# The triangular substitution of two delta-net heads on 32 partitions, in a new order of heads, scans and products

## The chip, the core and the metric

The kernel runs on one core of one Trainium2 chip. The metric is the device time of one execution in microseconds (us); lower is better. The engines are TensorE (PE in the profile; PEld are its weight loads), VectorE (DVE), ScalarE (ACT), GpSimd (POOL) and SyncE (SP), which issues the transfers. Each engine works through its own queue in order; semaphores hold an instruction back until what it needs is there.

## The reference

One decoder layer on 512 tokens of width 2048, all in float32: a norm, one projection that feeds three mixers (stick-breaking attention with 6 heads, 4 gated convolution groups, a gated delta net with 6 heads), an output projection, and an MLP. What the change touches is the delta net:

```python
def gated_delta_rule(q, k, v, g, beta):
    ...
    m = jnp.where(strict, jnp.einsum('bhnid,bhnjd->bhnij', k_beta, k) * decay, 0.0)
    eye = jnp.eye(C, dtype=f32)
    t_mat = lax.linalg.triangular_solve(eye + m, jnp.broadcast_to(eye, m.shape),
                                        left_side=True, lower=True, unit_diagonal=True)
    u = t_mat @ v_beta
    w = t_mat @ (k_beta * jnp.exp(g)[..., None])
    ...
    def step(state, xs):
        q_c, k_c, u_c, w_c, a_c, gl_c = xs
        v_new = u_c - w_c @ state
        o = q_c @ state + a_c @ v_new
        state = state * jnp.exp(gl_c)[..., None, None] + jnp.swapaxes(k_c, -1, -2) @ v_new
        return state, o
```

For every head and every chunk of tokens a unit triangular matrix is inverted, and then a scan runs over the chunks, each step on the state of the one before.

## The kernel before

Products of float32 matrices are made as three matmuls of rounded parts: `wload` (L94 to L104) loads a weight tile `raw`, ScalarE rounds it to `whi` (L102), VectorE takes the rest `wlo` (L103), and `mm3` (L108 to L110) multiplies `whi` and `wlo` with the parts of the activations. `raw`, `whi` and `wlo` have four buffers each. A whole product of 512 tokens and 128 columns is `gemm`: 4 weight tiles, 48 matmuls, one PSUM buffer `mm` out of three (`MMB`), held until its reader has evacuated it.

The delta net takes 128 tokens as a chunk, so 4 chunks a head (`NB`). Per head h:

- `gdn_in(h)`: three products (k, q, v), a convolution, norms, and the 128x128 matrices `MT` (to be inverted) and `AT` of each chunk. `kq` and `MT` have three buffers, so the fourth head in line waits for the end of the first one's scan.
- `gdn_base(h)` (L406 to L476): the sixteen 32x32 diagonal blocks of the four chunks are gathered through DRAM (`sm`, then `Bq`) so that each lies on one partition: 16 partitions, 1024 elements. There VectorE inverts all sixteen at once in 31 steps of two instructions (L429, L431), 62 instructions a head, of up to 256 elements a partition. The result goes through DRAM again (`sy`) to `Xc`, and five small rounds of 32x32 and 64x64 matmuls on PSUM tag `b`, each evacuated by ScalarE or VectorE, put the full inverse together in `MT`.
- `gdn_scan(h)` (after `gdn_kdec`): for each chunk a chain of matmuls on PSUM tag `s` and small rows: `s`, `bp` (VectorE, L491), `s`, `vn` (ScalarE, L496), `s`, `Sn` (VectorE, L504), and so on to the next chunk; then a norm of the head (L519 to L523) and transposes on PSUM tag `o` (L526).
- `gdn_gate(h)`: one product for the output gate.

The four convolution groups (`sc_group(g)`, three products each) have no part in the delta net; they and the gates fill TensorE while VectorE inverts and scans. What the program says in sequence is not yet the order of the engines: a scheduler takes the instructions of the whole program with their priorities (base and scan are raised by `CPRIO` = 2000, weight loads by `WPRIO` = 400) and with its own estimates of time, and fixes the order of each engine's queue. The attention follows the delta net, with `sb_qk(0)` (two products) first.

Of the kernel before, what the change touches and what calls it, by code (L numbers as in the profile page):

```python
# [11 lines left out]
F32 = mybir.dt.float32  # L12
F32R = mybir.dt.float32r
AF = mybir.ActivationFunctionType
ALU = mybir.AluOpType

P = 128
T = 512
NB = T // P
# [15 lines left out]
CPRIO = 2000  # L35
# [18 lines left out]
def trunk(ctx, tc, xT, wv1, wv2, wa, wo, wu, wd, vec, wf, out, dbg=None):  # L54
    nc = tc.nc
# [126 lines left out]
    for k in range(KT):  # L182
# [3 lines left out]
        a = big()  # L186
# [50 lines left out]
    for c in range(2):  # L237
        t = tmp()
# [164 lines left out]
        V.tensor_tensor(out=q4(kdec), in0=q4(p), in1=edec[:, :, h:h + 1].broadcast_to([P, NB, P]), op=ALU.mult)  # L403
        heads[h]["kdec"] = kdec

    def gdn_base(h):  # L406


        MT = heads[h]["MT"]
        if not gb:  # L410
            gb.update(Bq=gt([P, 32, 32], "Bq"), Yq=gt([P, 32, 32], "Yq"), tq=gt([P, 256], "tq"),
                      Xc=gt([P, 256], "Xc"))
            G.memset(gb["Xc"], 0.0)
        Bq, Yq, tq, Xc = (gb[n] for n in ("Bq", "Yq", "tq", "Xc"))
        p0 = 32 * (h % 2)
        sm = dr.tile([P, NB, P], F32, name="sm", tag="sm", bufs=2)
        nc.sync.dma_start(out=sm, in_=q4(MT))
        for s in range(NB):
            nc.sync.dma_start(
                out=Bq[p0 + 4 * s:p0 + 4 * s + 4],  # L420
                in_=sm[32 * s:32 * s + 32, :, 32 * s:32 * s + 32].rearrange("a k b -> k a b"))
        B, Y, t = Bq[p0:p0 + 16], Yq[p0:p0 + 16], tq[p0:p0 + 16]
        Yf = Y.rearrange("p a b -> p (a b)")
        G.memset(Yf, 0.0)
        G.memset(Yf[:, 0:1024:33], 1.0)
        for i in range(31, 0, -1):
            n = 32 - i
            tv = t[:, :i * n].rearrange("p (a b) -> p a b", a=i)
            V.tensor_tensor(out=tv, in0=B[:, 0:i, i:i + 1].broadcast_to([16, i, n]),  # L429
                            in1=Y[:, i:i + 1, i:32].broadcast_to([16, i, n]), op=ALU.mult)  # L430
            V.tensor_tensor(out=Y[:, 0:i, i:32], in0=Y[:, 0:i, i:32], in1=tv, op=ALU.subtract)  # L431
        sy = dr.tile([16, 32, 32], F32, name="sy", tag="sy", bufs=2)
        nc.sync.dma_start(out=sy, in_=Y)
        Xv = q4(Xc)
        for s in range(NB):
            nc.sync.dma_start(
                out=Xv[32 * s:32 * s + 32, :, 32 * (s % 2):32 * (s % 2) + 32],
                in_=sy[4 * s:4 * s + 4].rearrange("k a b -> a k b"))
        X0 = gt([P, 256], "X0")
        V.transpose(out=X0, in_=Xc)  # L440
        p = xps("b")
        pv = q4(p[:, :128])
        for b in range(NB):
            for s in (0, 64):
                PE.matmul(pv[s + 32:s + 64, b], lhsT=q4(MT)[s:s + 32, b, s + 32:s + 64],
                          rhs=q4(X0)[s:s + 32, b, 0:32], start=True, stop=True)
        A1 = gt([P, 128], "A1")
        S.copy(out=A1[32:64], in_=p[32:64, :128])
        V.tensor_copy(out=A1[96:128], in_=p[96:128, :128])
        p = xps("b")  # L450
        pv = q4(p[:, :128])
        for b in range(NB):
            for s in (32, 96):
                PE.matmul(pv[s - 32:s, b], lhsT=q4(A1)[s:s + 32, b], rhs=Xv[s:s + 32, b, 32:64], start=True, stop=True)
        for s in (0, 2):
            r = slice(32 * s, 32 * s + 32)
            if s:
                V.tensor_scalar(out=Xv[r, :, 32:64], in0=pv[r], scalar1=-1.0, scalar2=None, op0=ALU.mult)
            else:
                S.mul(out=Xv[r, :, 32:64], in_=pv[r], mul=-1.0)  # L460
        lo, hi = slice(0, 64), slice(64, P)
        p = xps("b")
        for b in range(NB):
            PE.transpose(p[lo, b * 64:b * 64 + 64], Xc[lo, b * 64:b * 64 + 64], ident[lo, lo])
        X1 = gt([P, 256], "X1")
        S.copy(out=X1[lo], in_=p[lo, :256])
        p = xps("b")
        for b in range(NB):
            PE.matmul(q4(p[:, :256])[hi, b], lhsT=q4(MT)[lo, b, hi], rhs=q4(X1)[lo, b], start=True, stop=True)
        S.copy(out=X1[hi], in_=p[hi, :256])  # L470
        for r in (lo, hi):
            V.tensor_copy(out=q4(MT)[r, :, r], in_=Xv[r])
        p = xps("b")
        for b in range(NB):
            PE.matmul(q4(p[:, :256])[lo, b], lhsT=q4(X1)[hi, b], rhs=Xv[hi, b], start=True, stop=True)
        S.mul(out=q4(MT)[lo, :, hi], in_=q4(p[:, :256])[lo], mul=-1.0)  # L476
# [161 lines left out]
    def base(h):  # L638
        with tc.high_priority(CPRIO):
            gdn_base(h)  # L640

    def scan(h):
        with tc.high_priority(CPRIO):
            gdn_kdec(h)
            gdn_scan(h)

    gdn_in(0)
    base(0)
    gdn_in(1)
    scan(0)  # L650
    sc_group(0)
    base(1)
    gdn_in(2)
    scan(1)
    gdn_gate(0)
    base(2)
    gdn_in(3)
    scan(2)
    base(3)
    scan(3)  # L660
    gdn_in(4)
    base(4)
    gdn_gate(1)
    gdn_gate(2)
    gdn_in(5)
    scan(4)
    base(5)
    gdn_gate(4)
    sc_group(1)
    gdn_gate(3)  # L670
    sc_group(2)
    sc_group(3)
    scan(5)
    gdn.__exit__(None, None, None)
# [351 lines left out]
```

## Time and profile before

| what | us |
|---|---|
| median of 3 runs (lowest, highest) | 2260.18 (2259.96, 2262.76) |
| the profiled execution | 2259.93 |
| its span, first to last instruction | 2257.9 |
| mean granted TensorE clock, share of full speed | 0.995 |
| PEld, ACT, POOL busy | 1834.4, 914.6, 208.7 |
| DMA: mean over the span | 101 GB/s |

The page gives busy time and share of each engine, and the span in 40 equal slices of 56 us with a busy share in tenths. Tables by stretch give, for each stretch from A to B in us, its length and then busy time and count of each engine, the granted clock, the DMA share and GB/s. A row of the timeline is: start, duration, engine, line, operation, what is written <- what is read, shape, count, and in brackets how long the engine stood idle before it and what ended that. A group of instructions shows its count, busy time, mean in ns, and idle time before it. A wait is: who waited for whom, us in total, times, the longest.

The delta net lies at about 50 to 500 us, the attention at 500 to 780 us, the output projection and the MLP behind.

### The profile page before, as it was taken

How to read it: one execution, taken by the hardware profiler on the slowest of the kernel's cores; microseconds unless marked ns; L12 is line 12 of the kernel's file. 1: busy time of each engine (PE TensorE's matmuls, PEld its weight loads, DVE VectorE, ACT ScalarE, POOL GpSimd, SP SyncE). 2: the span in 40 equal slices, each digit the busy share in tenths (PEclk: the TensorE clock that was granted, in tenths of full speed). 3: DMA queues.
4: the chain of work that ended last, by engine and by line, in shares of the span. 5: the costliest groups of instructions: out<-in, count | busy, mean ns of one | idle time of the engine just before them, and what ended most of it. 6: DMA issues, size and time to landing. Idle time of an engine off the chain costs nothing.

```text
span 2257.9 us, 28036 instructions
## 1 busy us (share of the span) xinstructions
PE 2212.8 (98%) x10394; PEld 1834.4 (81%) x10394; DVE 1646.0 (73%) x2216; ACT 914.6 (41%) x1479; POOL 208.7 (9%) x205
## 2 busy tenths in 40 slices
PE   8999989999999999999999999999999999999998
PEld 7877777788989888788888888888888888888886
DVE  7798999854656743468787787787878878878774
ACT  5524544333434533433333333333333333333334
POOL 4323323101000111000000000000000000000003
PEclk9999999999999999999999999999999999999999
DMA  6332222333222343433433333333333243333332
GB/s 184 97 87 82 72 73 72 87 87 93 82 87 80 89 126 117 134 109 90 124 90 107 108 90 118 96 102 117 88 113 103 89 123 92 102 113 89 116 113 80
DMA packets 112504, 227.05 MB, mean 101 GB/s; under 512 B 18448, under 2 KB 20624, under 8 KB 112368
## 3 DMA queue, kind: packets, MB, share of 16 engines
q1 hardware_dynamic: 112368, 225.26, 33.8%
q8 instruction: 82, 1.34, 0.3%
q14 instruction: 54, 0.44, 0.1%
HBM read 218.53 MB, written 6.68 MB: 100 GB/s over the span
## 4 chain that ended last, share of the span: by engine, by line
PE 89%; DVE 7%; issue 1%; DMA 1%; ACT 1%; SPq 0%; POOL 0%; ACTq 0%; DVEq 0%; POOLq 0%
PE mm L108 19%; PE mm L109 19%; PE mm L110 19%; PE pp L110 8%; PE pp L108 8%; PE pp L109 8%; DVE Yq L431 2%; DVE tq L429 1%; DVE wlo L103 1%; PE mm L268 1%; PE mm L269 1%; PE mm L267 1%; DVE cv L337 1%; DVE big L189 0%; DMA xr<-in_xT_dram 0%
## 5 line engine op out<-in xcount | busy, mean ns | idle before, releaser
L102 ACT CAST whi<-raw 128x512 fp32r<-128x512 f32 (+1 forms) x544 | 333.0, 613 | 619.1 <-PE mm L109 569.5
L103 DVE TENSOR_TENSOR wlo<-raw,whi 128x512 fp32r<-128x512 f32 (+1 forms) x544 | 381.0, 701 | 233.4 <-ACT whi L102 227.3
L868 DVE TENSOR_TENSOR xq<-pp,xq 128x1024 f32<-128x1024 f32 x240 | 290.8, 1222 | 203.1 <-PE pp L110 200.6
L108 PE MATMUL mm<-big,whi 128*128 128x512 f32 x1024 | 406.4, 397 | 0.2 <-DVE y L558 0.2
L110 PE MATMUL mm<-big,wlo 128*128 128x512 f32 x1024 | 405.2, 396 | 0.2
L109 PE MATMUL mm<-big,whi 128*128 128x512 f32 x1024 | 404.4, 395 | 0.0
L108 PE MATMUL mm<-xw,whi 128*128 128x512 f32 x1024 | 398.8, 389 | 0.0
L110 PE MATMUL mm<-xw,wlo 128*128 128x512 f32 x1024 | 398.3, 389 | 0.0
L109 PE MATMUL mm<-xw,whi 128*128 128x512 f32 x1024 | 398.3, 389 | 0.0
L778 ACT CAST W<-q 128x1024 fp32r<-128x1024 f32 x210 | 220.8, 1051 | 399.4 <-PE pp L110 398.1
L108 PE MATMUL pp<-W,A 128*128 128x512 f32 x840 | 326.8, 389 | 0.0
L109 PE MATMUL pp<-W,A 128*128 128x512 f32 x840 | 326.8, 389 | 0.0
L110 PE MATMUL pp<-W,A 128*128 128x512 f32 x840 | 326.8, 389 | 0.0
L779 DVE TENSOR_TENSOR W<-q,W 128x1024 fp32r<-128x1024 f32 x210 | 255.5, 1216 | 5.3 <-ACT W L778 5.3
L110 PEld LDWEIGHTS mm<-big,wlo 128*128 128x128 f32 x1024 | 193.7, 189 | 40.6 <-DVE wlo L103 1.0
L108 PEld LDWEIGHTS mm<-big,whi 128*128 128x128 f32 x1024 | 194.0, 190 | 39.9 <-DVE y L558 0.4
L109 PEld LDWEIGHTS mm<-big,whi 128*128 128x128 f32 x1024 | 194.1, 190 | 39.7 <-DVE big L709 0.3
L108 PEld LDWEIGHTS mm<-xw,whi 128*128 128x128 f32 x1024 | 192.2, 188 | 40.3 <-issue 0.2
L109 PEld LDWEIGHTS mm<-xw,whi 128*128 128x128 f32 x1024 | 192.2, 188 | 40.1 <-issue 0.2
L110 PEld LDWEIGHTS mm<-xw,wlo 128*128 128x128 f32 x1024 | 192.0, 188 | 39.9
L110 PEld LDWEIGHTS pp<-W,A 128*128 128x128 f32 x840 | 157.8, 188 | 32.8
L109 PEld LDWEIGHTS pp<-W,A 128*128 128x128 f32 x840 | 157.6, 188 | 32.8
(264 smaller groups left out, 2226.3 us busy)
## 6 DMA issues: line engine op xcount, KB each, us to landing
raw<-in_wu_dram SPq DMA_DIRECT2D x256, 256.0 KB
q<-in_wd_dram SPq DMA_DIRECT2D x128, 512.0 KB
raw<-in_wa_dram SPq DMA_DIRECT2D x192, 256.0 KB
raw<-in_wo_dram SPq DMA_DIRECT2D x64, 256.0 KB
xr<-in_xT_dram SPq DMA_DIRECT2D x32, 256.0 KB
raw<-in_wv_dram SPq DMA_DIRECT2D x16, 256.0 KB
out_dram<-xq SPq DMA_DIRECT2D x16, 256.0 KB
raw<-in_wv_dram SPq DMA_DIRECT2D x16, 134.0 KB
```

What stands on the lines that cost most here:

```text
L102: S.copy(out=hi[:, :n], in_=raw[:, :n])
L103: V.tensor_tensor(out=lo[:, :n], in0=raw[:, :n], in1=hi[:, :n].bitcast(F32), op=ALU.subtract)
L108: PE.matmul(p, lhsT=lh, rhs=rh, start=first, stop=False, skip_group_check=more)
L109: PE.matmul(p, lhsT=lh, rhs=rl, start=False, stop=False, skip_group_check=more)
L110: PE.matmul(p, lhsT=ll, rhs=rh, start=False, stop=last, skip_group_check=more)
L267: PE.matmul(o, lhsT=xw[k][:, 0, s], rhs=hi[:, ws], start=k == 0 and b % 2 == 0, stop=False)
L268: PE.matmul(o, lhsT=xw[k][:, 0, s], rhs=lo[:, ws], start=False, stop=False)
L269: PE.matmul(o, lhsT=xw[k][:, 1, s], rhs=hi[:, ws], start=False, stop=k == KT - 1 and b % 2 == 1)
L431: V.tensor_tensor(out=Y[:, 0:i, i:32], in0=Y[:, 0:i, i:32], in1=tv, op=ALU.subtract)
L778: S.copy(out=o[:, 0], in_=src)
L779: V.tensor_tensor(out=o[:, 1], in0=src, in1=o[:, 0].bitcast(F32), op=ALU.subtract)
L868: V.tensor_tensor(out=x, in0=p, in1=x, op=ALU.add)
```

## The change

A new function `gdn_sub(h)` gathers the blocks of heads h and h + 1 into 32 neighbouring partitions, inverts all 32 blocks with one set of 62 instructions (32 partitions, the same elements per partition), and writes one `sy` for both. `gdn_base(h)` keeps what follows from `sy`. The calls are put in an order by pairs: two heads' `gdn_in`, then their `sub`, then bases and scans, with the gates and convolution groups moved between them. Lines from L436 of before on stand four lines later in the new file; the two instructions of the substitution (L429, L431) are now L428 and L430.

```diff
-    def gdn_base(h):
-        MT = heads[h]["MT"]
+    def gdn_sub(h):
...
-        p0 = 32 * (h % 2)
-        sm = dr.tile([P, NB, P], F32, name="sm", tag="sm", bufs=2)
-        nc.sync.dma_start(out=sm, in_=q4(MT))
-        for s in range(NB):
-            nc.sync.dma_start(
-                out=Bq[p0 + 4 * s:p0 + 4 * s + 4],
-                in_=sm[32 * s:32 * s + 32, :, 32 * s:32 * s + 32].rearrange("a k b -> k a b"))
-        B, Y, t = Bq[p0:p0 + 16], Yq[p0:p0 + 16], tq[p0:p0 + 16]
+        p0 = 32 * (h // 2 % 2)
+        B, Y, t = (gb[n][p0:p0 + 32] for n in ("Bq", "Yq", "tq"))
+        for g in range(2):
+            sm = dr.tile([P, NB, P], F32, name="sm", tag="sm", bufs=2)
+            nc.sync.dma_start(out=sm, in_=q4(heads[h + g]["MT"]))
+            for s in range(NB):
+                nc.sync.dma_start(
+                    out=B[16 * g + 4 * s:16 * g + 4 * s + 4],
+                    in_=sm[32 * s:32 * s + 32, :, 32 * s:32 * s + 32].rearrange("a k b -> k a b"))
...
-            V.tensor_tensor(out=tv, in0=B[:, 0:i, i:i + 1].broadcast_to([16, i, n]),
-                            in1=Y[:, i:i + 1, i:32].broadcast_to([16, i, n]), op=ALU.mult)
+            V.tensor_tensor(out=tv, in0=B[:, 0:i, i:i + 1].broadcast_to([32, i, n]),
+                            in1=Y[:, i:i + 1, i:32].broadcast_to([32, i, n]), op=ALU.mult)
             V.tensor_tensor(out=Y[:, 0:i, i:32], in0=Y[:, 0:i, i:32], in1=tv, op=ALU.subtract)
-        sy = dr.tile([16, 32, 32], F32, name="sy", tag="sy", bufs=2)
+        sy = dr.tile([32, 32, 32], F32, name="sy", tag="sy", bufs=2)
         nc.sync.dma_start(out=sy, in_=Y)
+        heads[h]["sy"], heads[h + 1]["sy"] = sy[0:16], sy[16:32]
+
+    def gdn_base(h):
+        MT, sy, Xc = heads[h]["MT"], heads[h]["sy"], gb["Xc"]
...
     gdn_in(0)
+    gdn_in(1)
+    sub(0)
+    sc_group(0)
     base(0)
-    gdn_in(1)
+    gdn_in(2)
     scan(0)
...
+    sub(4)
+    gdn_gate(3)
+    sc_group(2)
     base(4)
-    gdn_gate(1)
-    gdn_gate(2)
-    gdn_in(5)
     scan(4)
     base(5)
     gdn_gate(4)
-    sc_group(1)
-    gdn_gate(3)
-    sc_group(2)
     sc_group(3)
     scan(5)
```

The whole list of calls is now: in 0, in 1, sub 0, group 0, base 0, in 2, scan 0, base 1, gate 0, scan 1, in 3, sub 2, gate 1, group 1, base 2, in 4, scan 2, base 3, gate 2, scan 3, in 5, sub 4, gate 3, group 2, base 4, scan 4, base 5, gate 4, group 3, scan 5.

How this moves the engines' queues is seen at two places near the end of the delta net. The numbers behind the names tell one buffer from another; `s_` and `b_` are the PSUM buffers of scan and base, `mm_` those of the products. First TensorE, before, at the base of head 5 and the scan of head 4:

```order
L108 MATMUL mm_4696<-big_119,whi_4699 128x512
L109 MATMUL mm_4696<-big_119,whi_4699 128x512
L489 MATMUL s_3975<-Sn_3967,kq_3108 128x128
L110 MATMUL mm_4696<-big_119,wlo_4700 128x512
L108 MATMUL mm_4696<-big_143,whi_4699 128x512
L109 MATMUL mm_4696<-big_143,whi_4699 128x512
L110 MATMUL mm_4696<-big_143,wlo_4700 128x512
L454 MATMUL b_4110<-Xc_918,A1_4107 32x32 x8
L108 MATMUL mm_4696<-big_169,whi_4699 128x512
L109 MATMUL mm_4696<-big_169,whi_4699 128x512
L110 MATMUL mm_4696<-big_169,wlo_4700 128x512
```

The same place of the changed kernel, the base of head 4 with the scan that follows it and the base of head 5:

```order
L458 MATMUL b_4326<-Xc_1239,A1_4323 32x32 x8
L468 MATMUL b_4337<-ident_78,Xc_1239 64x64 x4
L473 MATMUL b_4344<-X1_4342,MT_3289 64x64 x4
L479 MATMUL b_4352<-Xc_1239,X1_4342 64x64 x4
L498 MATMUL s_4365<-y_3268,MT_3289 128x128
L503 MATMUL s_4369<-vn_4367,kdec_4358 128x128
L512 MATMUL o_4373<-vn_4367,y_3288 128x128
L493 MATMUL s_4376<-Sn_4371,kq_3078 128x128
L449 MATMUL b_4445<-X0_4443,MT_3905 32x32 x8
L498 MATMUL s_4380<-bp_4378,MT_3289 128x128
L458 MATMUL b_4457<-Xc_1239,A1_4454 32x32 x8
L503 MATMUL s_4384<-vn_4382,kdec_4358 128x128
```

Before, two or more product matmuls (and elsewhere some 20) stand between two steps; now the steps follow each other. This goes on for 37 rows, to the third chunk of head 5's scan, before the next product, `mm_5137`, begins.

Second VectorE. Before, at the end of head 5's substitution (`tq`, `Yq`), with the evacuations of a convolution group's first and second product (`tmp_4612<-mm_4539`, `tmp_4688<-mm_4615`):

```order
L431 TENSOR_TENSOR Yq_916<-Yq_916,tq_917 16x31
L545 TENSOR_TENSOR tmp_4612<-mm_4539,R_525 128x512
L103 TENSOR_TENSOR wlo_4673<-raw_4670,whi_4672 128x512
L440 STREAM_TRANSPOSE X0_4096<-Xc_918 128x256
L103 TENSOR_TENSOR wlo_4700<-raw_4697,whi_4699 128x512
L103 TENSOR_TENSOR wlo_4718<-raw_4715,whi_4717 128x512
L504 SCALAR_TENSOR_TENSOR Sn_3967<-Sn_3952,elast_576,s_3965 128x128
L515 SCALAR_TENSOR_TENSOR y_3298<-o_3969,posg_582,oi_3972 128x128
L449 COPY A1_4107<-b_4098 32x128
L103 TENSOR_TENSOR wlo_4736<-raw_4733,whi_4735 128x512
L550 TENSOR_TENSOR tmp_4688<-mm_4615,tmp_4612 128x512
```

Now, in the substitution of heads 4 and 5, with the evacuation of the second product of the last group (`tmp_4721<-mm_4648`) and of the third product of the group before it (`y_4229<-mm_4234`):

```order
L430 TENSOR_TENSOR Yq_1237<-Yq_1237,tq_1238 32x13x19
L428 TENSOR_TENSOR tq_1238<-Bq_1236,Yq_1237 32x240
L559 SCALAR_TENSOR_TENSOR y_4229<-tmp_4226,vc_70,y_4229 128x512
L430 TENSOR_TENSOR Yq_1237<-Yq_1237,tq_1238 32x12x20
L554 TENSOR_TENSOR tmp_4721<-mm_4648,tmp_4645 128x512
L559 SCALAR_TENSOR_TENSOR y_4229<-tmp_4226,vc_70,y_4229 128x512
L428 TENSOR_TENSOR tq_1238<-Bq_1236,Yq_1237 32x231
L430 TENSOR_TENSOR Yq_1237<-Yq_1237,tq_1238 32x11x21
L428 TENSOR_TENSOR tq_1238<-Bq_1236,Yq_1237 32x220
L430 TENSOR_TENSOR Yq_1237<-Yq_1237,tq_1238 32x10x22
L562 TENSOR_TENSOR y_4229<-mm_4234,y_4229 128x512
```

The evacuation of a second product stood behind the whole substitution before, among splits `wlo`; now two evacuations stand in the middle of one, with 22 substitution rows still to come behind the first of them and one split only in the 25 rows before them.

More of the change, by code (lines that the diff above doesn't have):

```diff
@@ L413, in gdn_base @@
             G.memset(gb["Xc"], 0.0)
-        Bq, Yq, tq, Xc = (gb[n] for n in ("Bq", "Yq", "tq", "Xc"))
-        p0 = 32 * (h % 2)
-        sm = dr.tile([P, NB, P], F32, name="sm", tag="sm", bufs=2)
-        nc.sync.dma_start(out=sm, in_=q4(MT))
-        for s in range(NB):
-            nc.sync.dma_start(
-                out=Bq[p0 + 4 * s:p0 + 4 * s + 4],
-                in_=sm[32 * s:32 * s + 32, :, 32 * s:32 * s + 32].rearrange("a k b -> k a b"))
-        B, Y, t = Bq[p0:p0 + 16], Yq[p0:p0 + 16], tq[p0:p0 + 16]
+        p0 = 32 * (h // 2 % 2)
[7 more added lines that the diff above has]
+                    in_=sm[32 * s:32 * s + 32, :, 32 * s:32 * s + 32].rearrange("a k b -> k a b"))
         Yf = Y.rearrange("p a b -> p (a b)")
@@ L645, in scan, with sub @@
             gdn_scan(h)
+    def sub(h):
+        with tc.high_priority(CPRIO):
+            gdn_sub(h)
     gdn_in(0)
+    gdn_in(1)
+    sub(0)
+    sc_group(0)
     base(0)
-    gdn_in(1)
+    gdn_in(2)
     scan(0)
-    sc_group(0)
     base(1)
-    gdn_in(2)
+    gdn_gate(0)
     scan(1)
-    gdn_gate(0)
+    gdn_in(3)
+    sub(2)
+    gdn_gate(1)
+    sc_group(1)
     base(2)
-    gdn_in(3)
+    gdn_in(4)
     scan(2)
     base(3)
+    gdn_gate(2)
     scan(3)
-    gdn_in(4)
+    gdn_in(5)
+    sub(4)
+    gdn_gate(3)
+    sc_group(2)
     base(4)
-    gdn_gate(1)
-    gdn_gate(2)
-    gdn_in(5)
     scan(4)
```

## The prediction

> **What bounds the kernel now.** I read the engine totals first, then the slices, then one table of stretches around the delta-net stage (about 50 to 500 us).
>
> ```profile
> PE 2212.8 (98%) x10394; PEld 1834.4 (81%) x10394; DVE 1646.0 (73%) x2216; ACT 914.6 (41%) x1479; POOL 208.7 (9%) x205
> ...
> PE   8999989999999999999999999999999999999998
> ...
> DVE  7798999854656743468787787787878878878774
> ```
>
> TensorE is busy 98% of the span, so little can be won. Its few weak slices after the start lie in the delta-net stage, just where VectorE shows 8 and 9. The table of stretches gives the size:
>
> ```profile
> core 0: us, PE busy (x) PEld busy (x) DVE busy (x) ACT busy (x) POOL busy (x), PEclk, DMA share, GB/s
> 50.00:150.00 100.00, 100.00 (x454) 82.88 (x454) 79.41 (x142) 49.86 (x96) 34.86 (x32) 1.00 0.31 92
> 150.00:225.00 75.00, 68.19 (x360) 52.89 (x359) 63.21 (x130) 30.09 (x60) 18.31 (x20) 0.95 0.31 88
> 225.00:300.00 75.00, 69.44 (x343) 55.20 (x341) 68.43 (x132) 35.27 (x69) 28.85 (x24) 1.00 0.27 75
> 300.00:350.00 50.00, 43.88 (x223) 35.22 (x223) 47.47 (x84) 24.72 (x51) 14.63 (x13) 0.97 0.22 64
> 350.00:425.00 75.00, 70.89 (x370) 57.19 (x371) 65.39 (x142) 32.46 (x67) 20.82 (x20) 0.95 0.29 82
> 425.00:525.00 100.00, 99.22 (x536) 81.46 (x536) 64.84 (x134) 34.18 (x72) 10.91 (x9) 1.00 0.32 87
> ```
>
> From 150 to 525 us TensorE idles 6.81 + 5.56 + 6.12 + 4.11 + 0.78 = 23.4 us. After its longer waits the granted clock falls: (1 - 0.95) x 75, (1 - 0.97) x 50 and (1 - 0.95) x 75 add up to 9.0 us. So at most **32.4 us** can be won here. The view of waits says who is late:
>
> ```profile
> PE s L494 <- DVE bp L491: 8.3, 4, 3.9
> PE b L445 <- DVE X L440: 5.2, 2, 3.5
> PE s L489 <- DVE Sn L504: 2.7, 2, 2.5
> ```
>
> VectorE's short scan and base rows stand in a queue full of substitution rows. Note also the last stretch, 425 to 525: the tail of the stage costs almost nothing (0.78 us), because products stand between its chain steps.
>
> **The change part by part.** First, the substitution itself:
>
> ```profile
> L103 DVE TENSOR_TENSOR wlo<-raw,whi 128x512 fp32r<-128x512 f32 x135 | 97.1, 720 | 36.0 <-ACT whi L102 32.0 <-ACT rtok L135 2.6 <-DMA raw<-in_wa_dram 0.3
> L431 DVE TENSOR_TENSOR Yq<-Yq,tq 16x31 f32<-16x31 f32 (+15 forms) x186 | 83.8, 450 | 4.6
> L429 DVE TENSOR_TENSOR tq<-Bq,Yq 16x31 f32<-16x31 f32 (+15 forms) x186 | 81.5, 438 | 10.1 <-DMA Bq<-sm 5.5
> ...
> L555 DVE SCALAR_TENSOR_TENSOR y<-tmp,vc,y 128x512 f32<-128x512 f32 x6 | 5.9, 1001 | 1.4 <-ACT y L553 1.4
> ...
> 139.63 0.41 DVE L431 TENSOR_TENSOR Yq<-Yq,tq 16x252 f32<-16x252 f32 x1
> ...
> 144.57 0.40 DVE L393 TENSOR_TENSOR y<-i,g 128x256 f32<-128x256 f32 x1
> ```
>
> A row of 252 elements on 16 partitions takes 0.41 us and one of 256 elements on 128 partitions 0.40 us, so 32 partitions cost what 16 do. Half of the 372 rows go: (83.8 + 81.5) / 2 = **82.7 us less on VectorE**. GpSimd loses three pairs of clears, and the SP queue issues 19 transfers for two heads where it issued 20; neither is waited for, so both count as nothing (if one were, 1 us each).
>
> So VectorE is no longer short in the middle of the stage, and there the 32.4 us go. What comes late next: a pair's substitution starts only when both heads' MT are there, and its VectorE rows still have to be through before the next transpose X. For heads 2 and 3 the order has 62 substitution rows (27.5 us at their means) and some 45 others (about 31 us at the durations used below) between those points, against some 64 us of products on TensorE: little to spare. I leave **5 us** of waits there and around heads 0 and 1 (bounds 0, if all of it is hidden, and 14, if the rows stretch as below).
>
> ```profile
> 148.70 0.31 DVE L429 TENSOR_TENSOR tq<-Bq,Yq 16x156 f32<-16x156 f32 x1
> ...
> 303.65 1.26 DVE L429 TENSOR_TENSOR tq<-Bq,Yq 16x156 f32<-16x156 f32 x1
> ...
> 303.18 1.56 POOL L131 TENSOR_TENSOR cv<-cv,sg 128x512 f32<-128x512 f32 x1 [4.95 <-ACT sg L130]
> ```
>
> A 156-element row takes 0.31 us, and 1.26 us while GpSimd runs; that is in the means of 438 and 450 ns, but falls unevenly.
>
> Second, the tail. `kq` and `MT` have three buffers, so head 5's rows wait for the end of head 2's scan, and the third substitution (heads 4 and 5) cannot start before. By then most products are spent. Three places follow.
>
> *Place (a), the product mm_4892.* In the VectorE rows shown above, the read that frees a PSUM buffer (`tmp_4721<-mm_4648`) now stands in the middle of the substitution. The `mm` tag has three buffers; the other two are held by mm_4234 (freed six rows later) and mm_4729 (freed far later). So mm_4892 waits for that row, and with it all of TensorE's queue, since it works in order: the second product, and then the base of head 4. The first substitution row itself waits for the transfers of MT; one split is queued behind it, and TensorE needs that only for the last quarter of mm_4729, 11 us on. Prices:
>
> ```profile
> 145.62 0.33 SPq L417 DMA_DIRECT2D sm<-MT  x1
> ...
> 151.01 0.20 DVE L429 TENSOR_TENSOR tq<-Bq,Yq 16x31 f32<-16x31 f32 x1 [0.84 <-DMA Bq<-sm]
> ...
> 143.77 0.39 PE L108 MATMUL mm<-big,whi 128*128 128x512 f32 x1
> ...
> 144.68 0.39 PE L109 MATMUL mm<-big,whi 128*128 128x512 f32 x1
> ...
> 306.06 0.35 DVE L504 SCALAR_TENSOR_TENSOR Sn<-Sn,elast,s 128x128 f32<-128x128 f32 x1
> ...
> 506.57 0.68 DVE L403 TENSOR_TENSOR kdec<-s,edec 128x512 f32<-128x512 f32 x1
> ...
> 163.60 0.63 PE L108 MATMUL mm<-big,whi 128*128 128x512 f32 x1
> 164.03 0.63 PE L109 MATMUL mm<-big,whi 128*128 128x512 f32 x1
> ```
>
> From the transfer of MT to the first substitution row pass 5.4 us. From that row to the freeing row VectorE has 40 substitution rows (x 0.444 = 17.8), 5 splits (x 0.72 = 3.6) and 10 others (L559 1.0, four like the 0.68 of kdec, five like the 0.35 of Sn: 5.5): 26.9 us. Together 32.3 us after MT. TensorE has 68 full products in that time (143.77 to 144.68 are four starts, 0.2275 us each: 15.5) and small ones of about 3.8 us, of which 1.5 precede MT: 17.8 us. **(a) = 14.5 us** (10 to 19: substitution rows at their shortest, or more of them beside GpSimd).
>
> *Place (b), base and scan of heads 4 and 5.* In the TensorE rows shown above, 37 small rows follow each other without one product. Each step goes TensorE, ScalarE or VectorE, TensorE:
>
> ```profile
> 506.69 0.63 ACT L519 ACTIVATE MT<-y 128x512 f32<-128x512 f32 x1 [0.42 <-DVE y L515]
> ...
> 507.35 0.69 DVE L521 TENSOR_REDUCE ss<-MT 128x4 f32<-128x512 f32 x1
> ...
> 507.84 0.39 PE L494 MATMUL s<-y,MT 128*128 128x128 f32 x2
> ...
> 508.38 0.36 ACT L496 ACTIVATE vn<-s,be 128x128 f32<-128x128 f32 x1
> 508.64 0.28 ACT L135 ACTIVATE ss<-ss,eps_c 128x4 f32<-128x4 f32 x1
> ...
> 508.79 0.49 PE L499 MATMUL s<-vn,kdec 128*128 128x128 f32 x2 [0.56 <-ACT vn L496]
> ...
> 508.96 0.20 ACT L137 ACTIVATE ss<-ss 128x4 f32<-128x4 f32 x1
> ```
>
> 508.79 - 507.84 = 0.95 us a step. I count 20 steps in a row (4 of the base, 10 of head 4's scan, 1 for kdec, 5 of head 5's): 19.0 us. Queues lengthen three of them: a split ahead of the base's evacuation (1.2), head 4's norm ahead of head 5's `vn` (2.3), and the last convolution rows (L559 twice, then GpSimd, then L562), which free the buffer of the next product mm_5137 (3.0). 25.5 us, less some 8.2 us that TensorE works on these rows in either kernel: **(b) = 17.3 us** (9 with steps of 0.85 and no queues, 21 if the second base lengthens the scan).
>
> *Place (c), the end of head 5's scan*, again with no product behind it (mm_5215 and the first attention rows need buffers and splits that VectorE does after the norm). Two steps, 1.9 us, and the norm (square 0.63, reduce 0.69, 0.28, 0.20, a product like the 0.68 us of kdec, two rows of 0.3 ahead of them and the hops): 3.9 us, less 1.1 us of own work: **(c) = 4.7 us** (3 to 7).
>
> The granted clock falls again after such stops:
>
> ```profile
> 306.46 0.49 PE L489 MATMUL s<-Sn,kq 128*128 128x128 f32 x2 [2.45 <-DVE Sn L504]
> ...
> 308.41 0.63 PE L109 MATMUL mm<-big,whi 128*128 128x512 f32 x1
> ```
>
> The 9.0 us of before lie behind four waits, 2.25 us each; the slow rows start every 0.43 us (163.60 to 164.03). Three stops: **6.8 us** (4.5 to 9).
>
> The Trainium skill, "TensorE: Matmul & The Clock Gate", Part 1 (the HAM clock gate), says that the clock halves after an idle window of about 3.4 us and comes back after about as long of steady work. By that page a stop would cost an estimated 1.7 us and the three 5.1, which would make the sum 1.7 us less. The trace has the halved rows, but the 2.45 us wait was followed by them too (0.63 us at 308.41), so the row decides.
>
> **Sum:** 2259.93 (the profiled execution: span 2257.9 and 2.0 around it; 0.25 below the median) - 32.4 + 5 + 14.5 + 17.3 + 4.7 + 6.8 = 2275.8, say **2276 us**.
>
> **The rivals.**
> *The relief outweighs the tail (faster).* VectorE's 82.7 us are certain. If TensorE's real loss is 40 instead of 32.4 us (small delays between matmuls that the table counts as busy), and the three tail places cost their lower bounds (10 + 9 + 3, clock 4.5, 2 us in the middle), the time is 2259.9 - 40 + 28.5 = 2248. It decides at a tail of some 33 us. For it: every wait quoted above is VectorE's. Against it: the tail's rows have no product between them, whatever VectorE does. Chance 0.13.
> *They cancel.* (a) halves, because the buffer comes free some 20 VectorE rows earlier than I count: 2276 - 7 and one clock stop less gives about 2267, and with (b) at 12 about 2261. Chance 0.13.
> *VectorE binds again.* The pairs' rows are stretched by GpSimd (1.26 for 0.31 us above) in the middle too: 14 us there instead of 5, (a) 19, (b) 21, (c) 7: 2259.9 - 32.4 + 14 + 47 + 9 = 2298. Chance 0.10. That 32 partitions take longer than 16, so that nothing is saved, belongs here (2259.9 + 43.3 and no relief, over 2300); the two rows of 0.40 and 0.41 us speak against it, 0.01 of the 0.10.
>
> **How the numbers follow.** The forecast, a tail dearer than the relief by 5 to 33 us, has 0.64. Anything within 0.2% (4.5 us) is about what a measurement of this kernel can tell from no change. Faster by more: the first rival and a quarter of the second, 0.16; same, the rest of the second but a little, 0.09; slower 0.75. The range leaves out the first rival (0.13) and the top of the third (some 0.07): 2258 to 2294.
>
> **What would show it.** Right: in the changed profile the waits of TensorE for `bp`, `X` and `Sn` between 150 and 400 us are nearly gone; 186 fewer VectorE rows at unchanged means; TensorE stands before a product that waits for the read of tmp (now L554) around 405 to 425 us; a stretch of some 25 us with few matmuls follows some 25 us later, with a granted clock under 1 behind it; then a short stop before the first attention scores. Wrong: no such hole, or a hole well under 10 us, or substitution rows with a mean well over 0.45 us.

## The result, and the profile after

| | us | runs |
|---|---|---|
| before: median (lowest, highest) | 2260.18 (2259.64, 2262.76) | 5 |
| after: median (lowest, highest) | 2279.85 (2279.71, 2280.51) | 5 |
| ratio, 95% interval | 1.0086 (1.0072 to 1.0099) | |
| after, the profiled execution; its span | 2280.46; 2278.4 | |

The changed kernel is 19.7 us slower; I had predicted 2276 us. The lines of its page and of its table of stretches that answer to those of before:

```profile
PE 2227.3 (98%) x10394; PEld 1848.1 (81%) x10394; DVE 1570.0 (69%) x2030; ACT 919.9 (40%) x1479; POOL 192.2 (8%) x199
...
PE   8999998988899999999999999999999999999998
...
DVE  7677477373565743457778788787777878878774
...
PEclk9999999987999999999999999999999999999999
```

VectorE has 76.0 us less to do, and the whole is longer. A slice is 57 us. TensorE's eights were in the sixth slice before; now they are in the seventh and from the ninth to the eleventh (456 to 627 us), and the clock has its dent in the ninth and tenth.

```profile
core 0: us, PE busy (x) PEld busy (x) DVE busy (x) ACT busy (x) POOL busy (x), PEclk, DMA share, GB/s
150.00:225.00 75.00, 75.00 (x386) 60.70 (x384) 61.36 (x112) 35.78 (x63) 19.38 (x21) 1.00 0.36 99
225.00:300.00 75.00, 75.00 (x391) 61.94 (x385) 35.53 (x61) 33.21 (x66) 16.04 (x16) 1.00 0.29 82
300.00:350.00 50.00, 45.72 (x209) 37.16 (x208) 45.37 (x83) 21.92 (x41) 10.51 (x11) 0.98 0.25 69
350.00:425.00 75.00, 70.42 (x375) 55.86 (x374) 45.25 (x76) 33.66 (x64) 21.61 (x20) 0.94 0.31 89
425.00:490.00 65.00, 65.00 (x316) 54.33 (x316) 30.23 (x62) 23.95 (x46) 8.77 (x7) 1.00 0.32 86
490.00:515.00 25.00, 16.23 (x67) 12.69 (x66) 23.23 (x54) 5.56 (x12) 2.74 (x3) 0.73 0.19 53
515.00:530.00 15.00, 15.00 (x81) 12.19 (x80) 5.82 (x17) 3.98 (x7) 0.00 (x0) 1.00 0.42 119
530.00:563.00 33.00, 26.25 (x158) 20.33 (x156) 11.53 (x26) 10.25 (x29) 2.53 (x2) 0.59 0.07 18
563.00:576.00 13.00, 12.66 (x53) 10.50 (x54) 3.58 (x8) 2.50 (x5) 0.00 (x0) 0.86 0.14 43
576.00:600.00 24.00, 17.94 (x73) 14.53 (x72) 11.37 (x19) 10.67 (x21) 1.17 (x4) 0.79 0.14 44
```

The reader is to see three things. From 150 to 300 us TensorE has no idle time left, where it had 12.4 us. From 300 to 425 it idles 4.28 + 4.58 us. And behind 490 us there are the three stops of the prediction, one behind the other, with a clock down to 0.59.

Busy time and clock overlap there (a slow matmul counts as busy, and a slow clock costs nothing while TensorE waits for another engine), so they can't be added. For the comparisons below I use **lost time**: from the start of one TensorE matmul to the start of the next, less what the first takes at full clock between products, summed over all matmuls of a stretch. Those prices are read from the traces: 0.2275 us for a 128x512, in proportion for fewer columns of rounded parts; 0.113 us for a 128x128 and 0.217 us for a 128x256 of unrounded float32; 0.10 us for a 64x64 and 0.036 us for a 32x32. Lost time counts idle time, a slow clock and small gaps once each.

| lost time, us | 150 to 475 us | 475 to 625 us |
|---|---|---|
| before | 37.9 | 2.7 |
| after | 15.4 | 44.3 |

The middle won 22.5 us and the tail lost 41.6, which makes 19.1 of the 20.5 us between the spans. (The expectations of the experiments were written with a coarser count, which read 50.8 and 22.1 us for the middle and 5.1 and 51.9 for the tail, before and after, so that both differences are 5 to 6 us larger there.)

### When the last head is ready

The next rows are of the timelines: TensorE's transposes that end a head's scan (`o<-ident,MT`), its last matmuls that make a head's matrices (`i<-kq`), and VectorE's substitution. Before:

```profile
290.36 0.18 DVE L431 TENSOR_TENSOR Yq<-Yq,tq 16x31 f32<-16x31 f32 x1
...
402.61 0.60 PE L526 MATMUL o<-ident,MT 128*128 128x128 f32 x4
...
420.67 1.03 PE L390 MATMUL i<-kq 128*128 128x256 f32 x4
...
561.23 0.60 PE L526 MATMUL o<-ident,MT 128*128 128x128 f32 x4
```

These are the end of head 2's substitution, the end of head 2's scan, head 5's matrices, and the end of head 5's scan. After, with the start of the second pair's substitution, and of the third's, added:

```profile
281.26 0.60 PE L530 MATMUL o<-ident,MT 128*128 128x128 f32 x4
...
303.07 0.20 DVE L428 TENSOR_TENSOR tq<-Bq,Yq 32x31 f32<-32x31 f32 x1 [1.11 <-DMA Bq<-sm]
...
367.05 0.18 DVE L430 TENSOR_TENSOR Yq<-Yq,tq 32x31 f32<-32x31 f32 x1
...
464.03 0.60 PE L530 MATMUL o<-ident,MT 128*128 128x128 f32 x4
...
476.10 1.89 PE L390 MATMUL i<-kq 128*128 128x256 f32 x8
...
483.94 0.20 DVE L428 TENSOR_TENSOR tq<-Bq,Yq 32x31 f32<-32x31 f32 x1 [2.06 <-DMA Bq<-sm]
...
582.75 1.11 PE L530 MATMUL o<-ident,MT 128*128 128x128 f32 x4 [3.42 <-DVE MT L527]
```

Read from above: head 0's scan ends at 281.26; head 3 needs its buffers, so the substitution of heads 2 and 3 starts at 303.07 and ends at 367.05, where head 2 alone had been through at 290.36. Head 2's scan ends 61 us later than before, head 5 needs that head's buffers, and its matrices come 55 us later. TensorE did not stand still in between: it worked through the products. Before, 523 product matmuls were left when head 5's matrices came; now 211 are. Against these stands a chain that still takes 106.7 us (476.10 to 582.75).

The end of head 5's scan is the end of the stage. In all fourteen kernels of this study what comes behind it takes the same within 3.5 us: span less stage end is 1693.2 to 1696.7 us. So a run is explained, but for those, once its stage end is. The table has, for each, when head 2's scan ended, when the first of head 5's matrices came (MT 5), the product matmuls left from there to the stage end, the stage end (all from TensorE's timeline), and the lost time. The kernel before, run again beside the experiments, had medians of 2259.4 to 2260.1 us, so times of different rows can be compared to about 1 us.

| kernel | median us | ratio to before (95%) | head 2 ends | MT 5 | left | stage end | lost 150-475 | lost 475-625 |
|---|---|---|---|---|---|---|---|---|
| before | 2260.18 | | 403 | 421 | 523 | 561.2 | 37.9 | 2.7 |
| after | 2279.85 | 1.0086 (1.0072, 1.0099) | 464 | 476 | 211 | 582.8 | 15.4 | 44.3 |
| e1 three single sets | 2266.21 | 1.0031 (1.0020, 1.0042) | 389 | 438 | 446 | 569.1 | 34.2 | 13.2 |
| e2 copied out by ScalarE | 2280.23 | 1.0091 (1.0074, 1.0108) | 463 | 475 | 211 | 582.6 | 15.6 | 45.2 |
| e3 four buffers | 2241.86 | 0.9920 (0.9906, 0.9935) | 401 | 404 | 459 | 545.6 | 1.7 | 22.4 |
| e4 four products later | 2274.53 | 1.0066 (1.0051, 1.0081) | 445 | 449 | 336 | 580.5 | 17.8 | 39.0 |
| e5 last pair single | 2268.46 | 1.0037 (1.0023, 1.0051) | 467 | 479 | 218 | 572.4 | 16.7 | 32.7 |
| e6 before, four buffers | 2264.73 | 1.0024 (1.0014, 1.0034) | 407 | 409 | 595 | 570.0 | 37.9 | 8.9 |
| e7 e3 and e4 | 2258.10 | 0.9990 (0.9981, 1.0000) | 431 | 372 | 636 | 560.8 | 19.2 | 19.6 |
| e8 e3 and e5 | 2243.51 | 0.9928 (0.9913, 0.9943) | 409 | 409 | 445 | 546.3 | 10.4 | 14.0 |
| e9 second pair single | 2257.33 | 0.9987 (0.9978, 0.9997) | 414 | 422 | 447 | 561.7 | 15.6 | 24.0 |
| e10 pairs 1+2, 3+4 | 2261.09 | 1.0003 (0.9994, 1.0013) | 392 | 415 | 482 | 564.5 | 18.6 | 21.8 |
| e11 e10, four buffers | 2252.07 | 0.9964 (0.9951, 0.9977) | 386 | 406 | 506 | 553.8 | 11.7 | 16.8 |
| e12 idle matmuls | 2282.84 | 1.0105 (1.0088, 1.0123) | 464 | 476 | 211 | 586.3 | 15.9 | 38.8 |

(In e12 the idle matmuls count as work, so its lost time is not comparable with the others.)

### The profile page after: what moved, and what is told of

It reads as the page before. It is cut to its first block, busy times and chain, and to the rows that moved or that the text cites. A ratio compares the mean times of both kernels' runs of the same rounds, so it can differ in the third digit from the quotient of the medians.

```text
span 2278.4 us, 27849 instructions
## 1 busy us (share of the span) xinstructions
PE 2227.3 (98%) x10394; PEld 1848.1 (81%) x10394; DVE 1570.0 (69%) x2030; ACT 919.9 (40%) x1479; POOL 192.2 (8%) x199
## 4 chain that ended last, share of the span: by engine, by line
PE 94%; DVE 4%; issue 1%; ACT 1%; DMA 1%; POOL 0%; SPq 0%; ACTq 0%; DVEq 0%; POOLq 0%
PE mm L108 21%; PE mm L110 21%; PE mm L109 21%; PE pp L110 8%; PE pp L109 8%; PE pp L108 8%; DVE wlo L103 1%; PE mm L268 1%; PE mm L269 1%; PE mm L267 1%; DVE tq L428 1%; DVE Yq L430 1%; DVE big L189 0%; PE i L390 0%; PE s L498 0%
## 5 line engine op out<-in xcount | busy, mean ns | idle before, releaser
L103 DVE TENSOR_TENSOR wlo<-raw,whi 128x512 fp32r<-128x512 f32 (+1 forms) x544 | 386.4, 711 | 294.5 <-ACT whi L102 285.0
```

The costliest lines, as they stand in the source:

```text
L103: V.tensor_tensor(out=lo[:, :n], in0=raw[:, :n], in1=hi[:, :n].bitcast(F32), op=ALU.subtract)
```

## The experiments

### e1: the new order without the pairs

```diff
     def gdn_sub(h):
...
-        p0 = 32 * (h // 2 % 2)
-        B, Y, t = (gb[n][p0:p0 + 32] for n in ("Bq", "Yq", "tq"))
         for g in range(2):
+            p0 = 32 * g
+            B, Y, t = (gb[n][p0:p0 + 16] for n in ("Bq", "Yq", "tq"))
...
-            V.tensor_tensor(out=tv, in0=B[:, 0:i, i:i + 1].broadcast_to([32, i, n]),
+                V.tensor_tensor(out=tv, in0=B[:, 0:i, i:i + 1].broadcast_to([16, i, n]),
...
+            heads[h + g]["sy"] = sy
```

> The calls stay in the changed kernel's order, but sub(h) inverts its two heads one after the other, each on 16 partitions: 186 VectorE rows (82.7 us) come back and nothing else. Theory (the relief in the middle comes from the pairs' shared rows; the tail from the order and the buffers): the 28.8 us that TensorE won between 150 and 475 us are lost again and the tail stays, so 2280 + 29 = 2309 us, up to 2325 if the freeing read at place (a) moves back by a whole set of rows. Rival (the price of the tail is the tie between two heads: base 4 waits for head 5's blocks): with single sets base 4 starts while head 5's rows still run, products stand between its steps again, and the tail falls by 20 to 35 us: 2270 to 2285 us. Second rival (the order alone is what costs, the rows are cheap): 2280 us with VectorE at 1650 us busy.

Measured: 2266.21 us. My theory (2309) fell: giving back 186 VectorE rows made the kernel 13.6 us faster. The rival had the direction, a tail 31.1 us shorter, and was too careful in the time. The rows take back most of the gain in the middle (34.2 us lost instead of 15.4), and head 2, which no longer waits for head 3, is done at 389 us. So of the 19.7 us, some 6 are the order's and 13.6 are the pairs' own, a win of 18.8 and a loss of 31.1 in lost time.

### e2: the read at place (a) moved to ScalarE

```diff
+        if g == 3:
+            ev = gt([P, 512], "ev")
+            S.copy(out=ev, in_=phh)
+            phh = ev
         V.tensor_tensor(out=u[:, 2:514], in0=phh, in1=c, op=ALU.mult)
```

> ScalarE copies the second product of the last group out of PSUM, so the read that frees its buffer no longer stands in VectorE's queue in the middle of the third substitution. Theory (the three places of the tail are separate terms, as in my sum): the stop at place (a) goes with its clock stop, 8 to 12 us: 2268 to 2272 us. Rival (the tail is one chain, from the MT of head 5 to the end of its scan, against a fixed number of products): the product runs earlier, and TensorE then stands as long before the base of head 4, which waits for the same substitution: 2277 to 2283 us.

Measured: 2280.23 us, the rival. The waits of TensorE from 480 to 600 us (for whom, us in total, times, longest), after:

```profile
PE mm L108 <- DVE tmp L554: 4.0, 1, 4.0
```

and in this run, where L566 is the next read of a product in VectorE's queue:

```profile
PE mm L108 <- DVE y L566: 8.2, 2, 7.2
```

The product ran earlier, and TensorE then stood before the next one. From 475 to 500 us 6.1 us less were lost, from 500 to 525 6.8 more. Place (a) is a real wait but not a term of its own: the chain behind it has a fixed length, and what is left to fill it does not grow.

### e3: a fourth buffer for the heads' matrices

```diff
-        kq = gt([P, NB, 2, P], "kq", bufs=3)
+        kq = gt([P, NB, 2, P], "kq", bufs=4)
...
-        AT, MT = ytile(1), gt([P, 512], "MT", bufs=3)
+        AT, MT = ytile(1), gt([P, 512], "MT", bufs=4)
...
-        return y_pool.tile([P, 512], F32, name="y", tag=f"y{i}", bufs=(10, 6)[i])
+        return y_pool.tile([P, 512], F32, name="y", tag=f"y{i}", bufs=(10, 8)[i])
...
-        l0 = sp_pool.tile([P, P], F32, name=name + "0", tag=name + "0", bufs=2)
+        l0 = sp_pool.tile([P, P], F32, name=name + "0", tag=name + "0", bufs=1)
```

> kq and MT get a fourth buffer and the tag that holds vtok and AT eight instead of six, so that head 5's rows no longer wait for the end of head 2's scan; two small attention buffers (sq0, sk0) go from two to one to make room. Theory (the buffers set the start of the third substitution): its first row comes 40 us earlier or more, base and scan of head 4 find products beside them, and of the 47 us that the tail costs 20 to 35 go: 2245 to 2260 us. Rival (VectorE sets it: the rows are only moved into a stretch in which VectorE is already at 9 tenths, 310 to 370 us): the waits for X and bp there grow by what the tail wins, 2270 to 2285 us.

Measured: 2241.86 us, 38 below the changed kernel, 3 below the theory's range, and faster than the kernel before (0.992). The rows of its timeline for head 2's scan, head 5's matrices, the first row of the third substitution and the stage end:

```profile
401.07 0.60 PE L530 MATMUL o<-ident,MT 128*128 128x128 f32 x4
...
404.27 1.89 PE L390 MATMUL i<-kq 128*128 128x256 f32 x8
...
412.49 0.20 DVE L428 TENSOR_TENSOR tq<-Bq,Yq 32x31 f32<-32x31 f32 x1 [1.25 <-DMA Bq<-sm]
...
545.55 1.12 PE L530 MATMUL o<-ident,MT 128*128 128x128 f32 x4 [3.42 <-DVE MT L527]
```

The third substitution starts 71 us earlier than in the changed kernel. The tail gives back 21.9 us, and the middle, where I expected no gain, another 13.7, since the second pair no longer waits for head 0's buffers either (head 3's matrices come at 259 us instead of 294). Which of the three tags needs its buffer most was not tried.

### e4: four products behind the third substitution

```diff
     gdn_gate(1)
-    sc_group(1)
     base(2)
...
-    gdn_gate(2)
     scan(3)
     gdn_in(5)
     sub(4)
+    gdn_gate(2)
     gdn_gate(3)
+    sc_group(1)
     sc_group(2)
```

> One gate and one convolution group (four products, 44 us of TensorE) are called behind the third substitution instead of in the middle; by the queue six products instead of four then follow the MT of head 5. Theory (the tail is dear because the products are spent): two products more, 21.8 us, cover as much of the chain: 2258 to 2265 us. Rival (products are conserved: what the tail wins the middle loses, since the second substitution and heads 2 and 3 have fewer beside them): 2275 to 2290 us, with the idle time of TensorE moved to 300 to 450 us.

Measured: 2274.53 us, between the two and at the rival's edge. The tail won 5.3 us and the middle lost 2.4; the stage end moved by only 2.3 us. One wait of the middle that grew is that of head 1's last transposes for VectorE, in the stretch of the second substitution: 10.4 us, where it was 2.8 (waits of TensorE, 300 to 520 us):

```profile
PE o L530 <- DVE MT L527: 14.2, 2, 10.4
```

### e5: only the last pair single

```diff
-    sub(4)
+    sub1(4)
+    sub1(5)
```

`sub1(h)` is the substitution of the kernel before for one head, without the part that follows `sy`.

> The changed kernel with one difference: heads 4 and 5 are inverted one after the other on 16 partitions (62 VectorE rows more), the first two pairs stay together. Theory (after the run with three single sets: the tail is dear because the base of head 4 is tied to the blocks of head 5, which wait for the end of head 2's scan; the shared rows help only in the middle): the middle keeps the changed kernel's loss of 22 us between 150 and 475 us, give or take 8 for the rows that come back, and the tail falls from 52 to about 17 us as with single sets: 2245 to 2255 us. Rival (the tail was shorter there only because the whole stage ran later on VectorE): 2262 us or more. Second rival (it was the order of products, which is the same here): 2275 to 2285 us.

Measured: 2268.46 us. My theory fell; the first rival's time held, but its reason was not tested. Base 4 was free of head 5, and that was worth 11.4 us (the tail lost 32.7 us, against 44.3 in the changed kernel and the 17 that I expected), but head 5 came as late as ever, because head 2 did:

```profile
467.35 0.60 PE L552 MATMUL o<-ident,MT 128*128 128x128 f32 x4
...
478.54 1.89 PE L390 MATMUL i<-kq 128*128 128x256 f32 x8
```

So the tie that costs most is not where the hole is.

### e6: four buffers without the pairs

The same four lines as e3, in the kernel before.

> The kernel before with the buffers of the run with four (kq and MT four, eight for vtok and AT, one each for sq0 and sk0), no pairs, old order. Theory (the fourth buffer pays only where two heads are tied; before, VectorE's rows set the waits, and its tail cost only 5 us): 2254 to 2262 us. Rival (more heads in flight help any order): 2238 to 2250 us, as with pairs.

Measured: 2264.73 us, 0.24% slower than before and 3 us above the theory's range; the rival fell. The buffers alone win nothing (the middle still loses 37.9 us), so the 38 us of e3 are the pairs and the buffers together. Why it is some 5 us slower was not followed up; the tail loses 6 us more.

### e7 and e8: the remedies together

e7 has the lines of e3 and e4, e8 those of e3 and e5.

> Pairs, four buffers, and the four products called behind the third substitution. Theory (with four buffers the loss that is left, 26 us behind 475 us, is still a chain without products, and the middle, with 12 us, has slack now): 5 to 12 us less than with the buffers alone, 2230 to 2237 us. Rival (products are conserved and the middle pays, as it did with three buffers, where the tail won 7 us and the middle lost 5): 2238 to 2248 us.

> Both remedies: four buffers, and heads 4 and 5 inverted one after the other. Theory (both cut the same tie between the base of head 4 and the end of head 2's scan, so they do not add): 2232 to 2243 us. Rival (they take away different waits and add, 18 us of the one and some 30 of the other below 2280, and the tail ends as in the kernel before): 2215 to 2230 us.

Measured: e7 2258.10 us, worse than its rival; e8 2243.51 us, just above the upper end of its theory. In e7 head 5's matrices are there at 372 us, earlier than anywhere else, and the stage still ends 15 us later than in e3: head 2's scan ends at 431 instead of 401. The waits of TensorE from 300 to 350 us have

```profile
PE s L493 <- DVE Sn L508: 6.7, 2, 3.7
```

where e3 has none of any kind. Head 2's scan is 30 us late because its substitution is 29 us late: in both kernels the set of heads 2 and 3 starts at 267.1 us, but it ends here first in e3, then in e7:

```profile
305.16 0.18 DVE L430 TENSOR_TENSOR Yq<-Yq,tq 32x31 f32<-32x31 f32 x1
```

```profile
334.37 0.18 DVE L430 TENSOR_TENSOR Yq<-Yq,tq 32x31 f32<-32x31 f32 x1
```

In e7 other VectorE rows stand between its rows, and head 1's `Sn` (at 334.59 us) stands right behind the last of them. Early matrices are needed, but are not enough: the scans ahead of the last one have to be early too. In e8 the two remedies cut the same tie: the tail wins 8.4 us more than in e3, and the middle, with 62 rows more on VectorE, loses 8.7.

### e9: only the second pair single

```diff
-    sub(2)
+    sub1(2)
+    sub1(3)
```

> The changed kernel with heads 2 and 3 inverted one after the other on 16 partitions; heads 0 and 1, 4 and 5 stay pairs. Theory (the dear pair is the second: head 2 waits there for head 3, its scan ends at 464 us where it ended at 403 before and at 389 with three single sets, head 5's matrices need its buffers and come at 476 instead of 422 and 438, and the products run out in between): head 5's matrices come at 435 to 450 us, the tail falls from 52 to under 30 us, the middle lies between the 22 us of all pairs and the 45 of none: 2255 to 2263 us. Rival (each pair has a like share in the 13.6 us that three single sets won): 2273 to 2278 us.

Measured: 2257.33 us, as the theory had it, for head 5 even a little better:

```profile
414.16 0.60 PE L552 MATMUL o<-ident,MT 128*128 128x128 f32 x4
...
422.20 1.89 PE L390 MATMUL i<-kq 128*128 128x256 f32 x8
```

Untying heads 2 and 3 is worth 22.5 us, although it puts 62 rows back on VectorE; the middle loses no more than in the changed kernel (15.6 us and 15.4). The other two pairs together pay, once this one is untied: with all three untied (e1) the time is 8.9 us higher than here.

### e10 and e11: other pairs

Heads 1 and 2, 3 and 4 are pairs, 0 and 5 alone; the calls are now in 0, sub1 0, base 0, in 1, in 2, scan 0, sub 1, group 0, base 1, in 3, scan 1, base 2, gate 0, scan 2, in 4, sub 3, gate 1, base 3, group 1, scan 3, in 5, sub1 5, base 4, scan 4, gates 2 and 3, group 2, base 5, gate 4, group 3, scan 5. e11 adds the four lines of e3.

> Pairs of other heads: 1 with 2 and 3 with 4, heads 0 and 5 alone, three buffers, the calls arranged to suit. Theory (which head waits for which sets the tail: now head 2 closes its pair instead of opening one, so its scan and with it head 5's buffers are early): head 2's scan ends before 400 us, the tail costs 10 to 20 us, and two shared sets keep 15 to 25 of the 29 us won in the middle: 2238 to 2250 us. Rival (any pair delays its first head, and the delay only moves to heads 1 and 3, then to 4 and 5): 2262 us or more.

> The pairs 1 with 2 and 3 with 4 and the four buffers. Theory (the fourth buffer paid because head 5 was late; it is not late here): within 5 us of the same pairs with three buffers. Rival (the buffer shortens any order with pairs by 20 us or more, as it did for the changed kernel and with a single last pair): 20 us or more below it, about 2220 us.

Measured: 2261.09 and 2252.07 us, each between its theory and its rival. In e10 head 2's scan did end before 400 us (392) and the middle kept 19.3 us of the gain, but the tail lost 21.8, not 10 to 20. The delay had moved: head 3, which now waits for head 4, ends its scan at 492 us (460 before).

```profile
492.44 0.66 PE L556 MATMUL o<-ident,MT 128*128 128x128 f32 x4
```

The fourth buffer was worth 9 us here, against 38 with the first pairing.

### e12: idle matmuls in the chain

```diff
+WARM = (4, 5)
...
+    def warm(h, p, n=256):
+        if h in WARM:
+            for j in range(2):
+                PE.matmul(p[:, 512 - n:], lhsT=onesR, rhs=xw[j][:, 0, :n], start=True, stop=True)
```

It is called behind every chain matmul of base (n = 256) and behind those of scan on tag `s` (n = 384).

> The changed kernel with two idle matmuls (128x384, rounded operands, results unused) behind each chain matmul of base and scan of heads 4 and 5, in columns of the same PSUM buffer that nobody reads. Theory (the steps of place (b) took 1.25 instead of 0.95 us because the clock stood at 0.50 from 540 to 565 us): the clock stays over 0.8 there, the steps fall to about 1.0 us, the first products behind it run at full speed, and the end of head 5's scan comes 4 to 9 us earlier: 2271 to 2276 us. Rival (a step's length is set by semaphores and ScalarE or VectorE, or an evacuation waits for the idle matmuls too): the steps stay at 1.2 us or grow, 2279 to 2290 us, whatever the clock does.

Measured: 2282.84 us, the rival. The clock did in the main what the theory said: in the stretches of the chain, after and then in this run,

```profile
540.00:550.00 10.00, 9.94 (x74) 7.96 (x73) 3.06 (x10) 2.90 (x9) 0.00 (x0) 0.50 0.00 0
```

```profile
540.00:550.00 10.00, 9.58 (x86) 7.73 (x86) 2.39 (x8) 2.79 (x9) 0.00 (x0) 0.80 0.02 3
550.00:570.00 20.00, 14.82 (x84) 10.82 (x82) 7.82 (x16) 5.63 (x16) 2.55 (x2) 1.00 0.00 0
```

But the evacuations waited for the idle matmuls too. One of this run's ScalarE rows, with what released it (L439 is the idle matmul):

```profile
552.57 0.37 ACT L513 ACTIVATE vn<-s,be 128x128 f32<-128x128 f32 x1 [1.54 <-PE s L439]
```

So most steps stayed at 1.2 to 1.4 us (from 551.63 to 552.99 it is 1.36). What a step takes at full clock without idle matmuls is seen in the changed kernel itself, under (b) below.

## Why the prediction was right, and where it was off

*VectorE's saving: right.* 186 rows went, and the rows that stayed are a little shorter than before (412 and 424 ns against 438 and 450). The groups of rows by line, 50 to 550 us:

```profile
L430 DVE TENSOR_TENSOR Yq<-Yq,tq 32x31 f32<-32x31 f32 (+15 forms) x93 | 39.4, 424 | 2.4
L428 DVE TENSOR_TENSOR tq<-Bq,Yq 32x31 f32<-32x31 f32 (+15 forms) x93 | 38.3, 412 | 6.4 <-DMA Bq<-sm 4.1
```

165.3 - 77.7 = 87.6 us, where I had 82.7.

*32.4 us to win, 5 of them left: too much relief, off in both sizes.* By lost time 37.9 us were there from 150 to 475 us and 15.4 are left, a gain of 22.5 against my 27.4. These 4.9 us, less the 1.7 by which the tail was cheaper than its terms, are most of the 4 us by which the forecast was short. The table of stretches undercounts a chain among products, because overlapping rows count as busy. That was the first rival's point, and its 40 us is what the rows give (39.5 from 150 to 525 us). And 5 us was too little for the second pair: idle time of 8.9 us and a clock of 0.98 over 50 us and 0.94 over 75 us (5.5) are at the upper bound of 14. The waits of TensorE from 150 to 400 us are now

```profile
PE b L449 <- DVE X L444: 4.3, 1, 4.3
PE o L530 <- DVE MT L527: 2.8, 1, 2.8
PE s L498 <- DVE bp L495: 1.0, 1, 1.0
```

`bp` fell to 1.0 us (6.3 of the 8.3 us of the prediction lie in this stretch) and `Sn` is gone, as foretold; `X` is not, with 4.3 us of 5.2 left. I had put 58.5 us of VectorE's rows into the second substitution and set them against 64 us of products; it took 64 us (303.07 to 367.05).

*The tail, 36.5 us and 6.8 for the clock: right in the sum.* It cost 41.6 us against 43.3. By place, in lost time:

| place | stretch, us | lost | predicted, with a clock stop of 2.25 |
|---|---|---|---|
| (a) | 486 to 515 | 13.0 | 16.75 |
| (b) | 530 to 576 | 20.4 | 19.55 |
| (c) | 576 to 600 | 9.8 | 6.95 |

(a) happened where it was described, VectorE's read in the middle of the substitution and TensorE behind it, but the wait for it is only a part of the loss:

```profile
502.30 1.11 PE L530 MATMUL o<-ident,MT 128*128 128x128 f32 x4 [3.08 <-DVE MT L527]
...
506.66 0.67 DVE L554 TENSOR_TENSOR tmp<-mm,tmp 128x512 f32<-128x512 f32 x1
...
507.38 0.80 PE L108 MATMUL mm<-big,whi 128*128 128x512 f32 x1 [3.97 <-DVE tmp L554]
```

The read came 22.7 us after the first substitution row, where I had 26.9. TensorE waited 3.97 us for it. In the 13 us ahead of it TensorE had already run out of products and stood 4.8 us in the end of head 3's scan (1.27, 0.46 and the 3.08 of the first row), which my sum had only as work; most of the rest is the clock, at 0.50 from 498.4 to 512.1 us. And all this stood at 507 us and not at 405 to 425: I had the place in the queue and not the time. And e2 says that its price isn't its own; the three places are one chain against a fixed number of products, and the sum came out in part because the chain's length is in it whichever way it is cut.

(b) came out near its price by luck, as two errors cancel. Its 37 rows took 31.2 us (532.15 to 563.34) where I had 25.5, and their own work is 12.5 us at the full-clock prices of lost time where I had 8.2. The steps took 1.25 us where I took 0.95 from the profile of before. Two steps there, and a later one of head 5's scan, each TensorE's row and TensorE's next row, with ScalarE's `vn` between them:

```profile
537.16 0.80 PE L498 MATMUL s<-y,MT 128*128 128x128 f32 x2 [0.47 <-ACT MT L480]
538.42 0.80 PE L503 MATMUL s<-vn,kdec 128*128 128x128 f32 x2 [0.46 <-ACT vn L500]
...
550.51 0.80 PE L498 MATMUL s<-bp,MT 128*128 128x128 f32 x2 [0.57 <-DVE bp L495]
551.76 0.80 PE L512 MATMUL o<-vn,y 128*128 128x128 f32 x2 [0.46 <-ACT vn L500]
...
577.67 0.49 PE L498 MATMUL s<-bp,MT 128*128 128x128 f32 x2 [0.44 <-DVE bp L495]
578.62 0.49 PE L512 MATMUL o<-vn,y 128*128 128x128 f32 x2 [0.46 <-ACT vn L500]
```

In the first two, at a granted clock of 0.50, the two matmuls take 0.80 us and the idle part is 0.46. In the last, where the clock is 1.00 from 577 to 579 us, the matmuls take 0.49, the idle part is the same 0.46, and the step is 0.95 us again. So the slow clock makes the longer step; e12 could not show it, because its idle matmuls lengthened the steps in another way. I had reckoned with a low clock only behind a stop, not inside the chain; 20 steps of 0.3 us are 6 us, about the 5.7 that the chain is longer. (c) cost 2.9 us more than its price: the wait for the norm is 3.42 us, the first attention product waits another 1.74, and the clock is at 0.50 from 580.4 to 590.6 us.

*The cause.* "Head 5's rows wait for the end of head 2's scan ... By then most products are spent" holds: MT 5, the 211 matmuls left, and e3. What I had not seen is why head 2's scan itself ends 61 us late, the tie to head 3 in the second pair (e9), and that this tie costs about twice what the last pair's does (22.5 us in e9, 11.4 in e5), although the hole lies beside the last.

*The rivals.* The relief did not outweigh the tail, nor did the two cancel. VectorE did bind in the second pair as the third rival had it, without the rest of that rival.

## What to carry to other kernels

When two chains are made to share instructions, ask first when the first of them now ends, and who waits for what it frees: a saving on the busy engine (here 88 us) is worth only what the end of the last chain moves. Write down, before and after, when the last chain's input is ready and how much work is left to cover it (here 421 us and 523 matmuls against 476 and 211), and check the pace of the chains ahead of it too, which decided in e7. A tie that costs can often be kept and its wait taken away elsewhere: with a fourth buffer the same pairs are 18 us faster than the kernel before.

## What the runs showed of the hardware that was not expected

The granted clock does not follow the busy column. In the changed kernel it fell to 0.50 at 536.0 us, 4 us behind the last product, with no idle time over 1.16 us since then, and stayed there for 27 us of chain, 10 of which have TensorE busy for 9.94 us with small matmuls. It rose again only when rows of 128x512 had run without a break from 563.34 to 566.7 us. With matmuls of 128x384 and 128x256 among the same chain (e12) it went back to 1.00 though TensorE was busy for only 14.82 of 20 us. In the traces of the kernel before and the changed kernel every stretch at 0.50 from 150 to 625 us lasts a whole multiple of 3.41 us: 6.8 and three times 3.4 us before; 3.4, 6.8, 13.7, 30.7 and 10.2 us after. The Trainium skill, "TensorE: Matmul & The Clock Gate", Part 1 (the HAM clock gate), says that the clock halves after an idle window of about 3.4 us and returns after about as long of steady work. The 3.4 us of the return agree; the fall does not, if an idle window is one without work, as a chain with short waits and small matmuls was enough here.
